# A two-layer retention and stick-breaking trunk: three runs of small moves in the order of issue

## The chip, the cores and the metric

The kernel runs on one core of a Trainium2 chip. A core has a matrix engine (TensorE, in profiles PE, with PEld for its weight loads), two elementwise engines (VectorE, DVE, and ScalarE, ACT), a general one (GpSimd, POOL) and SyncE (SP), which here only issues transfers (DMA). Each engine works through a queue of its own in a fixed order, and they wait for one another by semaphores. The metric is device time in microseconds (us), from start to end of one execution, lowest is best.

## The reference

One sequence of 1024 tokens of width 1024 passes through two layers in float32. Cut to what is computed:

```python
# layer 0: retention, 4 heads, q and k of 256, v and gate of 512 each
proj = rms_norm(h, g_pre) @ ret_w_in
q, k = rope(q), rope(k) * 256 ** -0.5
o = retention_chunkwise(q, k, v)          # sum over s <= t of gamma**(t-s) (q_t.k_s) v_s
o = (o - mean(o)) * rsqrt(var(o) + eps)   # per head and token
h = h + rms_norm((o * silu(g)) @ ret_w_out, g_post)
# one shared K and V from layer 0's output
k_sh, v_sh = split(rms_norm(h, g_kv) @ w_kv)
# layer 1: stick-breaking attention, 8 heads of 128 (values of 256)
q, g = split(rms_norm(h, g_sb) @ sb_w_in)
A[t, s] = sigmoid(z_ts) * prod(1 - sigmoid(z_tj) for s < j < t)   # s < t
h = h + rms_norm(((A @ v_sh) * silu(g)) @ sb_w_out, g_sbpost)
```

## The kernel before

**Arithmetic.** Every large product is done in a reduced matmul type with a split of each operand into a high and a low part: `split` (L514 on ACT takes the high part, L515 on DVE the rest), and `mm3` (L413 to L415) issues high x high, high x low and low x high into one PSUM bank. Tokens are worked in two halves of 512. The large input projections (classes `Feature` and `Values`) use a scheme of the Strassen kind: seven products, numbered 1, 2, 5, 6, 7, 3, 4, instead of eight block products, with sums and differences of the two token halves and of weight blocks as operands. A product of `Feature` comes in two pieces (e = 0, 1) of 4 x 3 matmuls, and a piece ends in additions (L888) or copies (L884) that empty its bank.

**Filling products.** A `Phase` lists products in an order, and makes the weight tiles (`whl`, 3 buffers) two ahead. At the end of both layers' projections a few products are left out of that list's main part and kept as `filler`: pieces that are dealt among the steps of the first heads, so that TensorE has work while a head waits. In layer A these are six pieces, product 2 of the projections of retention heads 1, 2 and 3, two pieces each: they give the first token half's queries of those heads, which go to DRAM (`qa`) and come back for the rotation. They add to sums kept in `sg` (heads 1 and 2, 4 buffers, which the gates' loads share) or `acc` (head 3). In layer C they are eight pieces: products 2 and 3 of the last two gate projections.

**Retention heads.** Eight head steps run, four heads for each token half. `Ret.scores` loads and rotates keys and queries (L635 to L638), turns the keys (`kt`, L648) and makes scores. `Ret.mix` makes the output blocks and the carried state and normalises each block: statistics on DVE (L731, L732, L734), reciprocal root on POOL, scaling on ACT (L750). `Ret.gate` multiplies with the gate (L766), transposes on TensorE (L770) and splits into `oT`. `outs` makes the output product of a head, in 16 half pieces, whose matmuls read all of that head's `oT`. In the loop of `layer_a` head n's mix and gate are merged with head n-1's output product and head n+1's scores; head 0 has no output product before it, and has the filler instead.

**Opening of layer C.** `P.marks` gives `first`, the number of the opening's chunks (20): products 1 and 2 of three key and query projections and of one value projection. Chunks 12 to 15 are product 1 of the values, 16 to 19 product 2, into banks po and pz. Work is hung at the end of chunks by number (`at`). The rest of the residual update and the row that scales the second token half (`c_stats`, L508) hang at chunks up to 14. `w_turn` has four steps, one for each quarter of the width: each scales the kept half with that row (L1566), makes sums and differences of token halves (L864, L865, L867, L868) and splits five results (L514, L515); product 5 of the values, chunk 20, reads the first (`oT`).

**Attention heads.** 16 head steps. `Att.rows` makes score rows (bank z, L1262 and L1263 on ACT, L1267 and L1268 on POOL, a scan L1270 and a product L1271 on DVE), `Att.mix` transposes them (L1298), splits them and multiplies them with values into banks po; its last step is the gate (L1326).

**What sets the order.** The program order isn't the order of the queues. At the end `arrange` takes all instructions, with a model of their times, and plans each engine's queue: `latest` gives each instruction a latest time, going back from the end, with TensorE's instructions chained in program order and each claim on a buffer chained to the reads of the tile that had it before; `place` then builds the queues from what is ready, earliest latest time first; `justify` takes new ranks from that plan, and of five rounds the one that ends first by the model is kept. Buffers of one tag are claimed in the order of first use in the program. So a move in program order changes TensorE's preferences and the claims on buffers, and what is ready at a time decides with them. The queues are fixed when the program is built; on the chip nothing is reordered.

Of the kernel before, what the change touches and what calls it, by code (L numbers as in the profile page):

```python
# [308 lines left out]
def trunk(ctx, tc, xT, wts, gains, trig, ident_in, cols, last_gain, out):  # L309
# [43 lines left out]
    def hl(tag):  # L353
        return S(tag, [2, 512], F32R)
# [191 lines left out]
    B, tabs = Ctx(), []  # L546
# [306 lines left out]
    def w_turn(raws, kept, scale):  # L853

        tags = {6: ["sgn", "sgn", "A", "ko"], 7: ["AT", "AT", "AT", "ko"], 4: ["v"] * 4}
        B.x1, B.T = [None] * 4, {n: [None] * 4 for n in (5, 6, 7, 4)}

        def make(kt):
            q = [raws[kt][:, 0], kept[kt][:, 0], raws[kt][:, 1], kept[kt][:, 1]]
            if kt == 0:  # L860
                B.late, B.far = S("qk", [4, 2, 512], F32R), S("oT", [4, 2, 512], F32R)
            scale(kt)
            B.x1[kt] = B.late[:, kt]
            V.tensor_tensor(q[0], q[1], q[0], ALU.subtract)  # L864
            V.tensor_tensor(q[1], q[3], q[1], ALU.subtract)  # L865
            split((B.x1[kt][:, 0, :], B.x1[kt][:, 1, :]), q[3])
            V.tensor_tensor(q[3], q[3], q[0], ALU.subtract)  # L867
            V.tensor_tensor(q[2], q[2], q[3], ALU.subtract)  # L868
            for n, r in ((5, q[0]), (6, q[3]), (7, q[1]), (4, q[2])):
                x = B.T[n][kt] = B.far[:, kt] if n == 5 else hl(tags[n][kt])  # L870
                split((x[:, 0, :], x[:, 1, :]), r)

        return [lambda kt=kt: make(kt) for kt in range(4)]
# [603 lines left out]
    def layer_a():  # L1477

        units = units_c()
        ready = units[3]  # L1480

        F, load, stats0, norm, later, stats1, scale = a_open()
        vg = [values_a(h, h < 2, F if h == 0 else None) for h in range(NH)]
        qk = [Feature(16 * h, None, put_raw(h), "last" if h else "", h and (lambda e, h=h: S("acc" if h == 3 else "sg", [512]),),
                      (None, "mb", "ma", "mb")[h]) for h in range(NH)]
        order = [(x, n) for x in vg[:2 + 1] for n in (1, 2)]
        opening = len(order)
        order += [(x, n) for x in [vg[2]] + vg[:2] for n in rest]
        order += [(x, n) for x in vg[2 + 1:] for n in full]
        qks = len(order)  # L1490
        order += [(qk[0], n) for n in full] + [(x, n) for x in qk[1:] for n in (1, 5, 6, 7, 3, 4)]
        fill = len(order)
        order += [(x, 2) for x in qk[1:]]
        P = Phase(order, (opening, qks, fill))
        first, kq, end, halt = P.marks
        at = P.at
        load[0]()
        at[0] += [late_constants] + load[1:4]
        at[1] += load[4:7]
        at[2] += load[7:]  # L1500
        for j, k in ((3, 0), (4, 1), (5, 2)):
            at[j].append(stats0[k])
        for j, k in zip((6, 6, 7, 7, 8, 9, 10, 11), range(8)):
            at[j].append(norm[k])
        for j, k in zip((8, 8, 9, 9, 10, 10, 11, 11), range(8)):
            at[j].append(later[k])
        for j, k in zip((12, 13, 14), range(3)):
            at[j].append(stats1[k])
        for j, f in zip((16, 18, 20, 21), w_turn(F.raws, F.kept, scale)):
            at[j].append(f)  # L1510
        at[first].append(lambda: trays.__setitem__(slice(None), ["sc0", "sc1", "A", "A", "A", "A"]))
        at[kq].append(lambda: ring.__setitem__(slice(None), ["wraw", "wraw", "wraw", "vo", "vo"]))
        heads = [Ret(t, h) for t in range(2) for h in range(NH)]
        sc = []
        for k in range(8):
            at[end - 4 + k // 2].append(lambda k=k: (sc or sc.extend(heads[0].scores()), sc[k]()))
        for f in P.pieces(0, end):
            f()
        filler = P.pieces(end, halt)
        ys, acc, kept, post, load = [], [], [], [], []  # L1520
        for n in range(8):
            H = heads[n]
            if n % 4 == 1:
                ys = []
            if n:
                pre, out = heads[n - 1].out(ys, acc if n == 4 else None)
                pre[0]()
            else:
                out = filler
                ring[:] = ["wraw"]  # L1530
            extra, late_extra, soon = [], [], [ready.pop(0) for _ in range(min(2, len(ready)))] if 0 < n < 7 else []
            if n == 5:
                post = a_post(0, y_d[0], acc)
            if 5 <= n < 7:
                extra = post[:6] if n == 5 else post[6:11]
            if n == 7:
                extra = post[11:] + c_stats(0)
                load = w_prep()
                late_extra = load[:4]
            sides = heads[n + 1].scores() if n < 7 else []  # L1540
            main = H.mix() + H.gate()
            merge(main, (out, 0, 1 if n else 3), (sides[:2], 0, len(main) - 5), (sides[2:], 5, 0), (extra, 1, 5 if n == 7 else 2), (late_extra, len(main) - 4, 0), (soon, 2, 3))
        acc = []
        pre, out = heads[7].out(ys, acc, kept)
        pre[0]()
        return units, out, load[4:], kept, a_post(1, y_d[0], acc, kept)

    def layer_c(units, out, load, kept, post):

        kq, gs, vs, _ = units  # L1550
        order = [(x, n) for x in kq[:3] + [vs[0]] for n in (1, 2)]
        opening = len(order)
        order += [(x, n) for x in [vs[0]] + kq[:3] for n in rest]
        order += [(x, n) for x in kq[3:] + [vs[1]] + gs[:2] for n in full]
        order += [(x, n) for x in gs[2:] for n in (1, 5, 6, 7, 4)]
        fill = len(order)
        order += [(x, n) for n in (2, 3) for x in gs[2:]]
        P = Phase(order, (opening, fill))
        first, end, halt = P.marks
        at = P.at  # L1560
        merge(out[:14], (load, 0, 2))
        P.ensure(1)
        merge(out[14:])

        def scale(kt):
            V.tensor_tensor(kept[kt][:], kept[kt][:], rowh[0][:].unsqueeze(1).broadcast_to([128, 2, 512]), ALU.mult)  # L1566
        post += c_stats(1)
        for j, k in zip((1,2,3,3,4,5,6,7,8,9,10,12,13,14), range(len(post))):
            at[j].append(post[k])
        for j, f in zip((first - 2, first - 1, first - 1, first - 1), w_turn(B.raws, kept, scale)):  # L1570
            at[j].append(f)
        trays[:] = ["sc0", "sc1", "A"]
        at[first].append(lambda: trays.__setitem__(slice(None), ["sc0", "sc1", "A", "A", "A", "A"]))
        at[first].append(lambda: ring.__setitem__(slice(None), ["wraw", "wraw", "wraw", "vo", "vo"]))
        pres = w_out()
        for k, f in enumerate(pres):
            at[first + 30 + (end - first - 30 - 28) * k // len(pres)].append(f)
        heads = [Att(t, p) for t in range(2) for p in range(NPAIR)]

        def rows_of(n):  # L1580
            return heads[n // 2].rows(n % 2) if n < 16 else []
        r0 = []
        for k in range(4):
            at[end - 4 + k].append(lambda k=k: (r0 or r0.extend(rows_of(0)), r0[k]()))
        for f in P.pieces(0, end):
            f()
        filler = P.pieces(end, halt)
        merge(heads[0].mix(0), (filler[:4], 0, 1))
        merge(rows_of(1), (filler[4:6], 0, 0))
        merge(heads[0].mix(1), (filler[6:], 0, 1), (rows_of(2), 0, 1))  # L1590
        ys, acc = [], []
        for n in range(2, 16):
            A = heads[n // 2]
            if n % 2 == 0:
                L = heads[n // 2 - 1]
                if n % 8 == 2:
                    ys = []
                pre, out = L.out(ys, acc if L.t == 0 and L.pr == 3 else None)
                pre[0]()
            extra = []  # L1600
            if n == 9:
                post = c_post(0, y_d[1], acc)
            if 10 <= n < 14:
                extra = post[3 * n - 30:3 * n - 27]
            if n == 15:
                extra, last = finish(1, heads[7], ys)
            merge(A.mix(n % 2), (out[8 * (n % 2):][:8], 0 if n % 2 else 1, 1), (rows_of(n + 1), 0, 1), (extra, 1, 1))
        last()
# [79 lines left out]
```

## Time and profile before

| what | value |
|---|---|
| median of 3 runs | 1631.67 us (1631.51 to 1632.08) |
| the profiled execution | 1631.42 us |
| its span, first to last instruction | 1629.4 us |
| mean granted clock of TensorE | 0.999 |
| DMA | 386.43 MB, mean 237 GB/s |

The profile is of one execution. Busy times are of instructions on an engine; a matmul's end is modelled, since matmuls are pipelined, so that the time from one start to the next is the pace, and a row's own duration is longer than that. In a row of the timeline stand the start, the duration, the engine, the line, the operation, the tile written and those read, the shapes and the count of merged instructions; in brackets the idle time of the engine ahead of it and what ended that. Tiles carry their tag's name (`pma`, `pmb`, `po`, `pz` are PSUM banks). A line can be a helper's: L515 is every split's low part, L360 every transfer.

### The profile page before, as it was taken

What the parts mean: (1) busy time and instruction counts of PE and PEld (TensorE: products, weight loads), DVE (VectorE), ACT (ScalarE), POOL (GpSimd) and SP (SyncE); (2) the same over time, 40 slices, a digit from 0 to 9 for tenths busy, and PEclk for the clock granted to TensorE, in tenths of its full rate; (3) what the DMA queues carried; (4) which work ended last, traced back from release to release, by engine and by line L of the source; (5) the groups of instructions that cost most, each with busy time, mean ns of one, the idle gap of its engine ahead of it and who ended that gap; (6) DMA issues with size and microseconds to landing.
All of it is one profiled execution on the core that took longest, in us unless ns stands there. A gap on an engine that the chain in (4) does not pass through costs nothing.

```text
span 1629.4 us, 22500 instructions
## 1 busy us (share of the span) xinstructions
PE 1620.4 (99%) x7659; PEld 1351.9 (83%) x7659; DVE 1219.4 (75%) x1956; ACT 803.8 (49%) x1535; POOL 122.7 (8%) x271
## 2 busy tenths in 40 slices
PE   9999999999999999999999999999999999999998
PEld 7888888888888888888878888888888888888887
DVE  8997866654668888887689877767658666878775
ACT  8553334433456555444356665566544433554432
POOL 0000000000012222221000000000001111010010
PEclk9999999999999999999999999999999999999999
DMA  8556765543387877784786788978337877869771
GB/s 319 188 179 247 249 212 186 209 141 135 110 277 229 308 262 271 247 286 147 246 273 224 258 312 289 342 279 308 119 127 262 305 276 264 281 212 333 251 273 52
DMA packets 175890, 386.43 MB, mean 237 GB/s; under 512 B 18080, under 2 KB 34592, under 8 KB 173216
## 3 DMA queue, kind: packets, MB, share of 16 engines
q1 hardware_dynamic: 175056, 383.93, 68.1%
q8 instruction: 60, 0.98, 0.2%
q10 hardware_dynamic: 720, 1.07, 0.2%
q14 instruction: 54, 0.44, 0.1%
HBM read 263.82 MB, written 121.11 MB: 236 GB/s over the span
## 4 chain that ended last, share of the span: by engine, by line
PE 97%; DMA 1%; ACT 1%; DVE 1%; issue 0%; SPq 0%; DVEq 0%; POOLq 0%; POOL 0%
PE pma L413 12%; PE pma L415 12%; PE pma L414 12%; PE pmb L413 9%; PE pmb L415 9%; PE pmb L414 9%; PE po L414 6%; PE po L415 6%; PE po L413 6%; PE pz L415 3%; PE pz L414 3%; PE pz L413 3%; PE pz L1298 2%; PE pz L770 1%; DMA wraw<-in_wts_dram 1%
## 5 line engine op out<-in xcount | busy, mean ns | idle before, releaser
L514 ACT ACTIVATE whl<-wraw 128x512 fp32r<-128x512 f32 x266 | 156.4, 625 | 180.8 <-issue 62.6
L515 DVE TENSOR_TENSOR whl<-wraw,whl 128x512 fp32r<-128x512 f32 x266 | 176.3, 687 | 86.8 <-ACT whl L514 82.6
L1270 DVE TENSOR_TENSOR_SCAN sgn<-sgn 128x128 f32<-128x128 f32 (+3 forms) x64 | 86.6, 1353 | 18.0 <-POOL sgn L1268 18.0
L515 DVE TENSOR_TENSOR AT<-pz,AT 128x512 fp32r<-128x512 f32 (+1 forms) x96 | 51.1, 551 | 48.1 <-ACT AT L514 47.6
L514 ACT ACTIVATE AT<-pz 128x512 fp32r<-128x512 f32 (+1 forms) x96 | 45.0, 492 | 67.9 <-PE pz L1298 66.9
L413 PE MATMUL pmb<-oT,whl 128*128 128x512 f32 x192 | 76.0, 396 | 0.0
L415 PE MATMUL pmb<-oT,whl 128*128 128x512 f32 x192 | 75.3, 392 | 0.0
L414 PE MATMUL pmb<-oT,whl 128*128 128x512 f32 x192 | 75.0, 391 | 0.0
L413 PE MATMUL pmb<-qk,whl 128*128 128x512 f32 x184 | 72.6, 394 | 0.0
L415 PE MATMUL pmb<-qk,whl 128*128 128x512 f32 x184 | 72.1, 392 | 0.0
L414 PE MATMUL pmb<-qk,whl 128*128 128x512 f32 x184 | 71.8, 390 | 0.0
L515 DVE TENSOR_TENSOR whl<-vo,whl 128x512 fp32r<-128x512 f32 x62 | 41.6, 687 | 34.8 <-ACT whl L514 34.6
L884 ACT ACTIVATE f<-pma 128x512 f32<-128x512 f32 x52 | 30.7, 595 | 51.2 <-PE pma L415 48.7
L514 ACT ACTIVATE whl<-vo 128x512 fp32r<-128x512 f32 x62 | 37.5, 624 | 33.4 <-PE pma L415 17.1
L413 PE MATMUL pma<-xh,whl 128*128 128x512 f32 x136 | 53.1, 391 | 0.0
L415 PE MATMUL pma<-xh,whl 128*128 128x512 f32 x136 | 53.1, 390 | 0.0
L414 PE MATMUL pma<-xh,whl 128*128 128x512 f32 x136 | 52.9, 389 | 0.0
L907 ACT ACTIVATE wraw<-wraw,gn 128x256 f32<-128x256 f32 x102 | 45.6, 497 | 12.7 <-DMA wraw<-in_wts_dram 11.6
L1267 POOL TENSOR_SCALAR_AFFINE_SELECT A<-A 128x128 f32<-128x128 f32 x32 | 11.0, 344 | 536.2 <-DMA ko<-k 396.0
L1263 ACT ACTIVATE sgn<-pz 128x512 f32<-128x512 f32 (+2 forms) x96 | 46.8, 489 | 0.0
L1262 ACT ACTIVATE xh<-pz 128x512 f32<-128x512 f32 (+3 forms) x48 | 23.6, 491 | 46.3 <-PE pz L415 46.1
L1262 ACT ACTIVATE A<-pz 128x512 f32<-128x512 f32 (+3 forms) x48 | 23.5, 490 | 42.0 <-PE pz L415 41.9
(580 smaller groups left out, 5138.3 us busy)
## 6 DMA issues: line engine op xcount, KB each, us to landing
wraw<-in_wts_dram SPq DMA_DIRECT2D x332, 256.0 KB, 3.8
whl<-w SPq DMA_DIRECT2D x56, 512.0 KB, 5.8
vo<-in_wts_dram SPq DMA_DIRECT2D x70, 256.0 KB, 4.3
xh<-k SPq DMA_DIRECT2D x32, 512.0 KB, 6.6
v<-v SPq DMA_DIRECT2D x32, 512.0 KB, 5.4
k<-A SPq DMA_DIRECT2D x21, 512.0 KB, 5.0
e<-whl SPq DMA_DIRECT2D x10, 1024.0 KB, 6.3
whl<-e SPq DMA_DIRECT2D x10, 1024.0 KB, 6.5
```

The lines of the kernel that those rows point to most:

```text
L413: MM(p, lh, rh, start=start, stop=False, **kw)
L414: MM(p, lh, rl, start=False, stop=False, **kw)
L415: MM(p, ll, rh, start=False, stop=stop, **kw)
L514: A_.activation(dst[0], src, AF.Copy)
L515: V.tensor_tensor(dst[1], src, f32(dst[0]), ALU.subtract)
L770: nc.tensor.transpose(pt[:, 128 * e:128 * e + 128], on[:, 128 * e:128 * e + 128], ident[:])
L884: A_.activation(c[:], p[:], AF.Copy)
L907: A_.activation(x, x, AF.Copy, scale=gcol(self.gains[col], 2 * (2 * i + k) + c))
L1262: A_.activation(a[:, o:o + ww], p[:, :ww], AF.Sigmoid)
L1263: A_.activation(n[:, o:o + ww], p[:, :ww], AF.Sigmoid, scale=-1.0)
L1270: V.tensor_tensor_scan(n[:, :W][:, ::-1], n[:, :W][:, ::-1], n[:, :W][:, ::-1], 1.0, ALU.mult, ALU.bypass)
L1298: nc.tensor.transpose(p[:, 128 * tb:128 * tb + 128], self.A[hh][tb][:, c0:c0 + 128], ident[:])
```

## The change

Three edits, each in the order of issue; no instruction is added or removed.

In `layer_a` the six filling pieces are dealt in another way: two are issued ahead of head 0's mix, one is merged into head 0's mix and gate, and the last three are put ahead of head 0's output product, in head 1's step. Before, all six were merged into head 0's step, one each behind steps 1, 2, 3, 5, 6 and 7 of its eleven (counted from 0).

```diff
                 pre, out = heads[n - 1].out(ys, acc if n == 4 else None)
                 pre[0]()
+                if n == 1:
+                    out = filler[-3:] + out
             else:
-                out = filler
+                out = filler[2:-3]
                 ring[:] = ["wraw"]
+                for f in filler[:2]:
+                    f()
```

In `layer_c` the four steps of `w_turn` hang at the last four chunks of the opening, 16 to 19, one each. Before, one hung at chunk 18 and three at 19.

```diff
-        for j, f in zip((first - 2, first - 1, first - 1, first - 1), w_turn(B.raws, kept, scale)):
+        for j, f in zip((first - 4,first - 3,first - 2,first - 1), w_turn(B.raws, kept, scale)):
             at[j].append(f)
```

In `layer_c`, too, the first six of its eight filling pieces are dealt three to the first attention head's mix and three to the second head's score rows. Before it was four and two. The last two stay in the second head's mix.

```diff
-        merge(heads[0].mix(0), (filler[:4], 0, 1))
-        merge(rows_of(1), (filler[4:6], 0, 0))
+        merge(heads[0].mix(0), (filler[:3], 0, 1))
+        merge(rows_of(1), (filler[3:6], 0, 0))
         merge(heads[0].mix(1), (filler[6:], 0, 1), (rows_of(2), 0, 1))
```

## The prediction

> **What bounds the kernel now.** I read the page first, then whom TensorE waited for, then a table of its busy time in stretches of 20 us, and last the timeline around each stretch that isn't full. From the page, its head, its first part and the chain that ended last by engine:
>
> ```profile
> span 1629.4 us, 22500 instructions
> PE 1620.4 (99%) x7659; PEld 1351.9 (83%) x7659; DVE 1219.4 (75%) x1956; ACT 803.8 (49%) x1535; POOL 122.7 (8%) x271
> PE 97%; DMA 1%; ACT 1%; DVE 1%; issue 0%; SPq 0%; DVEq 0%; POOLq 0%; POOL 0%
> ```
>
> TensorE (PE) is busy in 1620.4 of 1629.4 us, so 9.0 us of the span is all that a new order could fill, and the change is only a new order: it adds and removes no instruction. The waits of PE (line, releaser, total, times, longest) and the stretches that the change may touch (us, then busy PE, PEld, DVE, ACT, POOL, then the granted clock, DMA share and GB/s) say where those 9.0 us are:
>
> ```profile
> PE pz L386 <- DVE f L384: 1.7, 1, 1.7
> PE pma L413 <- ACT oT L514: 0.9, 1, 0.9
> PE po L413 <- DVE f L888: 0.3, 1, 0.3
> ...
> 60.00:80.00 20.00, 20.00 (x90) 16.57 (x89) 19.34 (x33) 12.66 (x22) 0.00 (x0) 1.00 0.41 131
> ...
> 480.00:500.00 20.00, 19.14 (x112) 16.30 (x111) 19.44 (x32) 11.96 (x23) 6.71 (x10) 1.00 0.63 194
> ...
> 840.00:860.00 20.00, 19.65 (x86) 15.72 (x85) 19.56 (x32) 11.40 (x21) 0.00 (x0) 1.00 0.46 172
> ...
> 1260.00:1280.00 20.00, 19.84 (x108) 16.72 (x107) 16.68 (x31) 9.05 (x24) 4.48 (x12) 1.00 0.92 330
> ...
> 1620.00:1640.00 20.00, 3.95 (x34) 3.71 (x33) 5.32 (x13) 1.75 (x6) 0.65 (x1) 0.90 0.14 53
> ```
>
> 1.7 us goes before the first matmul and about 5.4 us after the last (1629.4 - 1620.0 - 3.95): the change reaches neither. Inside, PE misses 0.86 us in 480:500 (the gate of retention head 0, part A below), 0.35 in 840:860 (the opening of layer C, part B) and 0.16 in 1260:1280 (the first attention heads, part C). Every edit has exactly one of these three holes behind it. Since everywhere else PE is full, a microsecond filled in a hole should come off the end, unless the new order opens another.
>
> **The change part by part.** A filling product is 12 matmuls of 128x512. Twelve such starts, in a stretch where PE waits for nothing, and one start after a group of transposes:
>
> ```profile
> 425.61 0.39 PE L413 MATMUL pmb<-oT,whl 128*128 128x512 f32 x1
> ...
> 428.33 0.39 PE L413 MATMUL pmb<-oT,whl 128*128 128x512 f32 x1
> ...
> 1238.47 0.47 PE L413 MATMUL pma<-xh,whl 128*128 128x512 f32 x1
> 1238.79 0.39 PE L414 MATMUL pma<-xh,whl 128*128 128x512 f32 x1
> ```
>
> So (428.33 - 425.61) / 12 = 0.227 us from start to start, 2.72 us a product, and 0.32 - 0.227 = 0.09 us more for each place where transposes break the stream.
>
> **A: three products kept for retention head 1.** The end of head 0 in the timelines of PE, DVE and ACT:
>
> ```profile
> 487.64 0.45 PE L415 MATMUL pmb<-xh,whl 128*128 128x512 f32 x1
> 487.93 0.60 PE L770 MATMUL pz<-ident,sgn 128*128 128x128 f32 x4
> 489.39 0.50 PE L413 MATMUL pma<-oT,whl 128*128 128x512 f32 x1 [0.86 <-ACT oT L514]
> 489.73 0.28 PE L413 MATMUL pz<-xh,xh 128*128 128x256 f32 x1
> ...
> 475.94 0.70 DVE L731 BATCH_NORM_STATS2 small<-po 128x6 f32<-128x512 f32 x1 [1.88 <-PE po L415]
> 479.42 0.17 DVE L732 BATCH_NORM_AGGREGATE small<-small 128x2 f32<-128x6 f32 x1
> ...
> 485.28 0.78 ACT L750 ACTIVATE sgn<-po,small,small 128x512 f32<-128x512 f32 x1
> 488.75 0.59 ACT L514 ACTIVATE oT<-pz 128x512 fp32r<-128x512 f32 x1
> ```
>
> The last block of head 0 is in PSUM at about 475.9, is normalised only at 485.28, turned at 487.93, split at 488.75, and only then can head 0's output product start (489.39). Before that, PE runs out: the sixth and last filling product ended with the row at 487.64. The hole is worth the idle 0.86 plus the late next start (489.73 - 489.39 - 0.227 = 0.11), so **1.0 us**. The edit issues two products ahead of head 0, one inside it, and three behind its gates. What follows on PE is the same work; what changes is the priority: the planner ranks PE by program order, so the gates' transposes no longer stand behind the last products, and these are what is left to run while the last block is normalised. The chain from 475.9 to 489.3 is 13.4 us long though its own steps (0.70, 0.17, 0.78, 0.60, 0.59 and the like) are some 5; the rest is queueing behind head 1's work, so 1 us can be found. I take the whole 1.0 us. Bounds: 0 (the products are used up as early as before) and -1.0.
>
> Costs that are hidden. Call the six products f0 to f5, two each for heads 1, 2 and 3. Keeping f3 back holds one of the 4 sg buffers longer, so the fourth gate's load must take the buffer of the first. It is needed at the L766 of 486.16, and the first gate reads its own 17 us sooner:
>
> ```profile
> 468.82 0.68 DVE L766 TENSOR_TENSOR sgn<-sgn,sg 128x512 f32<-128x512 f32 x1
> 486.16 0.68 DVE L766 TENSOR_TENSOR sgn<-sgn,sg 128x512 f32<-128x512 f32 x1
> ...
> sg<-ga SPq DMA_DIRECT2D x11, 256.0 KB, 3.6
> S<-q SPq DMA_DIRECT2D x10, 256.0 KB, 4.4
> ...
> 515.89 0.60 ACT L651 ACTIVATE vo<-pz 128x512 fp32r<-128x512 f32 x1 [1.18 <-PE pz L648]
> ```
>
> At 3.6 us a load that is free. The result of f3 goes out over SP's queue and comes back for head 2's rotation; moved by two or three products (5 to 8 us) and with 4.4 us a transfer it is back near 495 to 500, while head 2's keys are turned only at 515 (the L651 above). SP issues in its planned order, so a store that isn't ready holds what is behind it: the next weight loads, which have six wraw buffers of lead. With more than some 15 us of delay head 2 would start late. The weight tile (whl, 3 buffers) of f2 and f3 is held longer too, and the second output unit waits for it: that unit is first read four half products (5.4 us) into the output product, which itself starts behind f3. All three at nothing.
>
> **B: sums asked for sooner.** The four steps of w_turn move in program order from chunks 18, 19, 19, 19 to 16, 17, 18, 19. Their DVE work and the place where PE waits:
>
> ```profile
> 831.01 2.36 DVE L1566 TENSOR_TENSOR v<-v,acc 128x1024 f32<-128x1024 f32 x2 [1.33 <-ACT acc L508]
> 847.61 0.68 DVE L515 TENSOR_TENSOR oT<-A,oT 128x512 fp32r<-128x512 f32 x1
> 848.21 0.68 DVE L888 TENSOR_TENSOR f<-po,f 128x512 f32<-128x512 f32 x1
> 849.41 0.68 DVE L888 TENSOR_TENSOR f<-po,f 128x512 f32<-128x512 f32 x1
> ...
> 845.61 0.39 PE L415 MATMUL po<-whl,xh 128*128 128x512 f32 x1
> 848.33 0.39 PE L415 MATMUL pz<-whl,xh 128*128 128x512 f32 x1
> 849.03 0.47 PE L413 MATMUL po<-whl,oT 128*128 128x512 f32 x1 [0.32 <-DVE f L888]
> 849.54 0.50 PE L414 MATMUL po<-whl,oT 128*128 128x512 f32 x1
> ```
>
> From 848.33 two starts take 0.70 and 0.51 where 0.227 each is the pace: 0.47 + 0.28 = **0.75 us**. They wait for two L888, which empty the po banks and stand behind the sums in DVE's full queue: the last matmul into po ended at 846.0, the first L888 began at 848.21, right after a split. The sums can't begin sooner than the row that scales them (L508 ends at 831.0, DVE takes L1566 at once), so the edit moves claims on buffers and the planner's ranks, not data; the steps issue no DMA. The two additions could have run 2 us sooner ahead of a split (oT of the fourth step) whose reader comes three chunks (36 matmuls, 8.2 us) later, so there is room to get it right, and nothing in the edit that forces it: between 0 and -0.75 I take half, -0.4. The other way, the third step's A buffer is now claimed ahead of the value store of chunk 19, which may hold that store and its f buffer; six f buffers stand between that and PE, so I cost it at nothing.
>
> **C: products dealt 3-3.** One product (f3) moves from the first attention head's mix to the score rows of the second. The hole behind:
>
> ```profile
> 1274.05 0.45 PE L415 MATMUL pmb<-oT,whl 128*128 128x512 f32 x1
> 1274.54 0.33 PE L413 MATMUL pz<-xh,xh 128*128 128x128 f32 x1
> ...
> 1275.09 0.41 PE L1298 MATMUL pz<-ident,A 128*128 128x128 f32 x2
> 1275.62 0.39 PE L413 MATMUL pz<-xh,xh 128*128 128x256 f32 x1
> ```
>
> 0.49 instead of 0.227, and 0.53 instead of two transposes and their break (2 x 0.11 + 0.09 by the row above): 0.26 + 0.22, so **0.5 us**. It lies 30 us behind the moved product, with a whole mix between, and is a wait for a score's bank and operands, not for a filling product. The product's loads, weight tile and stores move by less than 3 us with it, and no other part of this stretch has a hole that they could widen. Half again: -0.25; bounds 0 and -0.5.
>
> **New order elsewhere.** All queues behind an edit are planned anew; one to three transpose breaks more or fewer (0.09 each) and a new hole of the size of the smaller ones: between -0.3 and +0.7, taken as +0.3.
>
> Sum: -1.0 - 0.4 - 0.25 + 0.3 = -1.35. The profiled execution took 1631.42 us (2.0 around its span), 0.25 below the median of the runs, 1631.67; on the median that gives 1630.3, and I say **1630.4**.
>
> **The rivals.**
> 1. The holes stay or come back beside their old place (the plan is a list of readiness, and a filling product that is ready is still used whenever the rest isn't): 1631.7, within 1631.2 to 1632.4. For it: the three products were ready and were used before the gates because the mix of head 0 has waits of its own. Chance 0.33.
> 2. All three holes close and nothing opens: 1631.67 - 1.0 - 0.75 - 0.5 = 1629.4. Chance 0.07.
> 3. Slower: PE's queue is fixed when the program is built, so a transpose of a gate (L770) that stands ahead of the kept products blocks them if its input is late. Place: 476 to 489, where head 0's last block took 9.3 us to L750. Up to three products, 8.2 us, would then stand behind the wait; it decides once over 4.3 us of them do (3.3 net of part A). Then 1635 to 1639. Against it: the planner puts what is ready first, and other heads' scores lie between. Chance 0.05; a smaller loss of the kind, 1632.4 to 1635, 0.04. [...]
> 4. Much faster: the pace itself would have to change. [...] A new order could still save breaks: 3.3 us less 2.25 from the holes is twelve breaks of 0.09, all gained. Chance 0.01.
>
> The forecast has 0.50 (1629.6 to 1631.2). 0.2%, about what a measurement of this kernel can tell from no change, is 3.3 us: more than all three holes together (2.25). So faster 0.01, same 0.94, slower 0.05. The range 1629.2 to 1632.2 takes in rival 2, most of rival 1 and the forecast, over 8 in 10.
>
> **What would show it.** A: no PE wait for oT before head 0's output product, kept products between the last L770 and it. B: no PE wait on L888 near 848, both L888 ahead of the last oT split. C: PE 20.00 in 1260:1280. Matmul count 7659 and clock 1.00 as before. I am wrong if PE's idle time inside the span rises above 1.4 us, or falls without the span doing so.

## The result and the profile after

| | before | after |
|---|---|---|
| median | 1631.91 us (22 runs, 1631.22 to 1635.22) | 1629.36 us (22 runs, 1628.69 to 1631.11) |
| span of the profiled execution | 1629.4 us | 1626.7 us |

The ratio is 0.9983, 95% interval 0.9977 to 0.9988: 2.55 us less by the medians, a small gain that lies inside the 0.2% called "same" in the prediction and inside its range, but below its forecast's band (1629.6 to 1631.2), and twice what it forecast. From the page of the changed kernel, the same three lines as before:

```profile
span 1626.7 us, 22505 instructions
...
PE 1619.3 (100%) x7659; PEld 1351.5 (83%) x7659; DVE 1219.1 (75%) x1956; ACT 804.1 (49%) x1535; POOL 122.1 (8%) x271
...
PE 98%; DMA 1%; DVE 0%; issue 0%; ACT 0%; SPq 0%; DVEq 0%; POOLq 0%; POOL 0%
```

The matmuls are the same 7659, and outside PE's busy time 7.4 us are left of 9.0. The waits of PE in the changed kernel:

```profile
PE pz L386 <- DVE f L384: 1.7, 1, 1.7
PE pma L414 <- DVE whl L515: 0.2, 1, 0.2
PE pma L415 <- DVE xh L515: 0.2, 1, 0.2
```

The waits for oT (L514) and on L888 are gone. The three stretches, and the last one (us, busy PE, PEld, DVE, ACT, POOL, clock, DMA share, GB/s):

```profile
480.00:500.00 20.00, 20.00 (x106) 17.06 (x105) 19.06 (x33) 11.51 (x21) 5.66 (x10) 1.00 0.78 275
840.00:860.00 20.00, 20.00 (x89) 16.25 (x88) 19.50 (x32) 12.15 (x24) 0.00 (x0) 1.00 0.41 150
1260.00:1280.00 20.00, 20.00 (x112) 17.46 (x112) 12.92 (x24) 8.96 (x23) 3.92 (x12) 1.00 0.85 297
1620.00:1640.00 20.00, 1.41 (x13) 1.17 (x11) 3.06 (x7) 0.51 (x2) 0.65 (x1) 0.94 0.11 41
```

PE is full in all three, and has 1.41 us of work past 1620 instead of 3.95: 2.54 us came off the end.

Busy time hides part of a hole, because a matmul's modelled end runs over the next one's start (a row of 512 columns is 0.39 us long, and the next starts after 0.227). A sharper count is PE's **lost time**: for each matmul, the time to the next start less the pace of its width (0.227 us for 512 columns, 0.174, 0.119 and 0.11 for 384, 256 and 128), summed over a stretch. It counts the breaks at transposes too, so only differences matter. The heads of the columns are the stretches, in us from the start; the entries are us:

| kernel | 2:40 | 465:500 (A) | 843:852 (B) | 1268:1278 (C) |
|---|---|---|---|---|
| before | 3.21 | 0.98 | 0.91 | 0.95 |
| after | 3.01 | 0.05 | 0.27 | 0.17 |

That is -0.93 for A, -0.64 for B, -0.78 for C, and -0.20 from the first 40 us, which the change doesn't touch: 2.55 of the 2.7 us between the spans. No new hole stands against it in this execution, which is the fastest of the 22.

**A.** Rows of PE, ACT and DVE of the changed kernel:

```profile
487.13 0.39 PE L413 MATMUL pmb<-xh,whl 128*128 128x512 f32 x1
487.35 0.39 PE L413 MATMUL po<-A,sc 128*128 128x512 f32 x1
...
488.95 0.60 PE L770 MATMUL pz<-ident,sgn 128*128 128x128 f32 x4
...
491.23 0.39 PE L414 MATMUL pmb<-xh,whl 128*128 128x512 f32 x1
...
484.25 0.78 ACT L750 ACTIVATE sgn<-po,small,small 128x512 f32<-128x512 f32 x1
...
489.58 0.60 ACT L514 ACTIVATE oT<-pz 128x512 fp32r<-128x512 f32 x1 [2.06 <-PE pz L770]
...
469.82 1.21 DVE L635 TENSOR_TENSOR S<-S,tab 128x1024 f32<-128x1024 f32 x1
```

Head 0's chain did not end earlier. Its last block is normalised 1.0 us sooner (L750 at 484.25 instead of 485.28), but the transposes of that gate stand behind kept products and head 1's output blocks in PE's queue (488.95), and its last split is at 489.58, where it was at 488.75. What changed is that PE still has work then. Kept products run up to 487.13 and again from 491.23, two matmuls, and head 1's output blocks (po<-A) already run at 487.35: head 1's query comes earlier (the rotation L635 at 469.82), because the two products that make it are issued ahead of head 0. In the timeline of the kernel before, that rotation was

```profile
476.56 1.21 DVE L635 TENSOR_TENSOR S<-S,tab 128x1024 f32<-128x1024 f32 x1
```

**B.** The same kernel near 848:

```profile
846.38 0.68 DVE L888 TENSOR_TENSOR f<-po,f 128x512 f32<-128x512 f32 x1
...
847.34 0.40 PE L413 MATMUL po<-whl,oT 128*128 128x512 f32 x1
...
847.58 0.68 DVE L888 TENSOR_TENSOR f<-po,f 128x512 f32<-128x512 f32 x1
847.71 0.50 PE L414 MATMUL po<-whl,oT 128*128 128x512 f32 x1
...
849.97 0.68 DVE L515 TENSOR_TENSOR oT<-A,oT 128x512 fp32r<-128x512 f32 x1
```

Both L888 are now ahead of the last oT split. One late start is left: 847.34 to 847.71 is 0.37 where 0.227 is the pace.

**C.** Where small score matmuls and transposes followed one another late before, 512-wide products stand between them now:

```profile
1274.08 0.47 PE L413 MATMUL po<-AT,v 128*128 128x512 f32 x1
1274.40 0.39 PE L414 MATMUL po<-AT,v 128*128 128x512 f32 x1
1274.63 0.40 PE L415 MATMUL po<-AT,v 128*128 128x512 f32 x1
1274.86 0.34 PE L413 MATMUL pz<-xh,xh 128*128 128x384 f32 x1
1275.04 0.40 PE L413 MATMUL pma<-oT,whl 128*128 128x512 f32 x1
```

### The profile page after: what moved, and what is told of

It is laid out like the page before. It is cut to its first block, busy times and chain, and to the rows that moved or that the text cites. A ratio compares the mean times of both kernels' runs of the same rounds, so it can differ in the third digit from the quotient of the medians.

```text
span 1626.7 us, 22505 instructions
## 1 busy us (share of the span) xinstructions
PE 1619.3 (100%) x7659; PEld 1351.5 (83%) x7659; DVE 1219.1 (75%) x1956; ACT 804.1 (49%) x1535; POOL 122.1 (8%) x271
## 3 DMA queue, kind: packets, MB, share of 16 engines
q10 hardware_dynamic: 720, 1.07, 0.2%
## 4 chain that ended last, share of the span: by engine, by line
PE 98%; DMA 1%; DVE 0%; issue 0%; ACT 0%; SPq 0%; DVEq 0%; POOLq 0%; POOL 0%
PE pma L413 12%; PE pma L415 12%; PE pma L414 12%; PE pmb L413 9%; PE pmb L415 9%; PE pmb L414 9%; PE po L414 6%; PE po L415 6%; PE po L413 6%; PE pz L414 3%; PE pz L415 3%; PE pz L413 3%; PE pz L1298 2%; PE pz L770 1%; PE pz L488 0%; DMA wraw<-in_wts_dram 0%
## 5 line engine op out<-in xcount | busy, mean ns | idle before, releaser
L514 ACT ACTIVATE whl<-wraw 128x512 fp32r<-128x512 f32 x266 | 156.2, 625 | 175.1 <-issue 62.6
L515 DVE TENSOR_TENSOR whl<-wraw,whl 128x512 fp32r<-128x512 f32 x266 | 176.1, 686 | 87.0 <-ACT whl L514 84.4
L515 DVE TENSOR_TENSOR AT<-pz,AT 128x512 fp32r<-128x512 f32 (+1 forms) x96 | 51.1, 551 | 50.0 <-ACT AT L514 49.6
L514 ACT ACTIVATE AT<-pz 128x512 fp32r<-128x512 f32 (+1 forms) x96 | 45.1, 492 | 68.4 <-PE pz L1298 67.9
L515 DVE TENSOR_TENSOR whl<-vo,whl 128x512 fp32r<-128x512 f32 x62 | 41.7, 689 | 35.1 <-ACT whl L514 34.8
L884 ACT ACTIVATE f<-pma 128x512 f32<-128x512 f32 x52 | 30.7, 595 | 49.7 <-PE pma L415 49.3
L514 ACT ACTIVATE whl<-vo 128x512 fp32r<-128x512 f32 x62 | 37.5, 624 | 34.7 <-PE pma L415 17.5
```

Source lines behind the costliest of these rows:

```text
L514: A_.activation(dst[0], src, AF.Copy)
L515: V.tensor_tensor(dst[1], src, f32(dst[0]), ALU.subtract)
L884: A_.activation(c[:], p[:], AF.Copy)
```

## The experiments

The theory after the result: each edit closes the hole behind it (A and C leave work for PE there, B lets DVE empty the banks sooner), and the three gains add. Rivals: the parts need one another; part A only moves its hole; another piece of an edit does the work than the one supposed. The kernels compute the reference in full; only the order differs, and in one of them a buffer. A theory's number holds within its own text. Medians (of 11 runs) are beside 33 runs of the kernel before on the same chip: its median was 1632.28 us for A, B, C and the hoist alone, 1632.01 for the pairs and for the step of the sums, 1632.26 for two kept products, the changed kernel once more, the other buffer and the 2-4 deal.

**Part A alone.** The first diff above, without the others.

> Only the retention edit (two products ahead of head 0, one inside, three kept for head 1); layer C as before. Theory 1, each edit closes the hole behind it and the effects add: TensorE's 0.86 us wait for oT near 488 is gone, the holes near 848 (0.75 us) and 1274 (0.5 us) are as before; span 1.0 to 1.1 us below before, ratio 0.9993 to 0.9994. Rival, the whole plan is made anew by any edit and the gain belongs to none of them alone: the holes near 848 or 1274 change too, and the span falls by something else than 1.0 us.

Measured: 1631.48 us, ratio 0.9997 (0.9988 to 1.0006); the span of its profile is 1629.5 us, and not the 1.0 us less that theory 1 expected. The wait for oT is gone, but there is another. From its waits of PE:

```profile
PE po L413 <- ACT sc L709: 0.5, 1, 0.5
PE po L413 <- DVE f L888: 0.3, 1, 0.3
```

And its timeline of ACT:

```profile
472.17 0.60 ACT L709 ACTIVATE sc<-po 128x512 f32<-128x512 f32 x1 [1.56 <-DMA st<-sc]
```

L709 copies a block of head 0's carried state into `sc`, of which there is one buffer, and SP stores it. The copy of the second block waits here until the store of the first has landed, holds a po bank meanwhile, and PE waits for that bank. Up to layer C each engine's queue in this program is the changed kernel's own, and there the same copy waited for nothing but PE (0.83 us). So it was open whether this belongs to the change or to this execution; more executions of the same queues had to tell.

**Part B alone.** The second diff.

> Only the sums of w_turn asked for sooner. Theory 1: the hole near 848 shrinks from 0.75 us to about 0.15, as in the changed kernel; the other two stay (0.86 us wait near 488 exactly as before); span 0.6 us less, ratio 0.9996. Rival: the edit moves no data and the hole near 848 closes only because everything ahead of it was planned anew by the retention edit; then this kernel has the hole still, ratio 1.0000.

Measured: 1631.85 us, ratio 0.9998 (0.9990 to 1.0007). Lost time at B 0.30 against 0.91; the wait for oT (0.9) and the hole at C are as before. The first 40 us lost 1.4 us more than in the profile of the kernel before, which hides the 0.6 in the span (1630.0). The hole still closes without part A, so the rival (it closes by what was planned ahead of it) falls.

**Part C alone.** The third diff.

> Only the 3-3 deal of the first attention heads. Theory 1: TensorE is full from 1260 to 1280, the late starts of 0.5 us are gone and some 0.3 us more by fewer breaks at transposes; span 0.8 us less, ratio 0.9995. Rival: the hole near 1274 stays or is replaced by another of its size, ratio 1.0000, since the gain in the changed kernel came from the new plan ahead of it.

Measured: 1631.59 us, ratio 0.9997 (0.9988 to 1.0006), span 1628.6, the 0.8 us less that theory 1 expected. Lost time at C 0.13 against 0.95; A and B are not closed (1.15 and 0.87).

**The hoist without the kept products.** Is it the two products ahead of head 0 that close A's hole, or those kept behind it?

```diff
-                out = filler
+                out = filler[2:]
+                for f in filler[:2]:
+                    f()
```

> Half of the retention edit: two products ahead of head 0, the other four merged into head 0 as before, none kept. If the gain of part A is the earlier queries of head 1 (its rotation, scores and mix come sooner and fill the wait), the 0.86 us wait is gone here too, span 1.0 us less, ratio 0.9994. If it is the products kept back, the wait stays at 0.5 to 1 us and the ratio is 0.9998 to 1.0000.

Measured: 1634.13 us, ratio 1.0009 (1.0000 to 1.0018), above the kernel before. The wait of PE that replaces the one for oT:

```profile
PE pz L770 <- DVE sgn L766: 1.7, 1, 1.7
```

Its timeline:

```profile
488.62 0.77 ACT L750 ACTIVATE sgn<-po,small,small 128x512 f32<-128x512 f32 x1
489.52 0.68 DVE L766 TENSOR_TENSOR sgn<-sgn,sg 128x512 f32<-128x512 f32 x1
490.32 0.42 PEld L770 LDWEIGHTS pz<-ident,sgn 128*128 128x128 f32 x4 [1.85 <-issue]
490.35 0.63 PE L770 MATMUL pz<-ident,sgn 128*128 128x128 f32 x4 [1.74 <-DVE sgn L766]
```

With nothing kept, PE comes to the last gate's transpose 1.7 us before its input is there. This is a wait of the kind of the prediction's third rival, in the gate it named, with no kept products behind it; it comes with the hoist and goes with the kept products. Neither alternative of the expectation was right: the hole did not close and did not stay, it grew. The two products that make head 1's query are ahead of head 0 here too, so an early query alone isn't enough. In that stretch the granted clock stayed at 1.00.

**Two products kept instead of three.**

```diff
-                    out = filler[-3:] + out
+                    out = filler[-2:] + out
...
-                out = filler[2:-3]
+                out = filler[2:-2]
```

> Part A with two of the six products kept instead of three; the third is merged into head 0's step, parts B and C left out. Theory 1 (what counts is how many matmuls are left on TensorE until head 0's first oT is split): in the changed kernel the split ended at 490.2 and the kept products at 491.5, so with one product less (2.72 us) TensorE runs out 1.3 to 2.0 us early, the wait for oT or for a transposed gate near 488 comes back at 1 to 2 us, and the time is 0.3 to 1.3 us above the kernel before. Theory 4 (the two products ahead of head 0 and the free gates do it, the number kept doesn't matter): no wait near 488 and 0.8 to 1.05 us below the kernel before.

Measured: 1633.25 us, ratio 1.0003 (0.9995 to 1.0012). Its wait of PE at 492.64:

```profile
PE po L413 <- ACT sgn L750: 1.2, 1, 1.2
```

The profile is of the longest of its eleven executions (1634.79 us), so its span says little.

A hole of the expected size came back, for another reason than the two named: PE waits for a po bank that ACT's scaling of a block has still to empty. The theory that the number kept doesn't matter falls by that wait; the median, 0.99 us above the kernel before where it wanted 0.8 us or more below, points the same way, though its interval reaches that far. Four products kept wasn't tried, nor three kept without the hoist.

**The parts in pairs.**

> Parts A and B, the attention products left 4-2. Theory 1 (each edit closes the hole behind it, the gains add): TensorE has no wait for oT near 488 and none on L888 near 848 beyond 0.25 us, the stretch 1260 to 1280 is as before (19.84), and the time is 1.05 + 0.60 = 1.65 us below the kernel before. Theory 2 (part A moves its hole, as in the run of A alone, where TensorE waited 0.47 us for ACT's L709 at 472): that wait is there again, and the time is about 0.1 + 0.6 = 0.7 us below. Theory 3 (the parts need one another): something between 2.0 and 2.7 us below.

> Parts A and C, the sums of token halves left where they were. Theory 1: no wait near 488, 20.00 busy in 1260 to 1280, the wait on L888 near 848 as before (0.3 us in the waits), and the time 1.05 + 0.85 = 1.9 us below the kernel before. Theory 2: the wait for L709 at 472 is there again, about 0.1 + 0.85 = 0.95 us below. With the run of A and B this gives two more executions of the same queues up to 500 us: if the wait at 472 comes in some and not in others, it goes by when the state's store lands and not by the plan.

> Parts B and C, the retention products left as before. Theory 1: the wait for oT near 488 is 0.9 us as before, the two other holes are closed, and the time is 0.60 + 0.85 = 1.45 us below the kernel before. Theory 3 (the parts need one another): less than 1.0 us below, with a hole of 0.3 us or more that neither part alone had.

Measured: A and B 1630.41 us (ratio 0.9990, 0.9981 to 0.9999); A and C 1630.64 (0.9991, 0.9982 to 1.0000); B and C 1630.62 (0.9991, 0.9982 to 0.9999). Lost time in us, worked out as above, in the profiles whose stretches lie at nearly the same times:

| kernel | 2:40 | 465:500 (A) | 843:852 (B) | 1268:1278 (C) |
|---|---|---|---|---|
| A | 3.42 | 1.05 | 0.88 | 0.99 |
| B | 4.65 | 0.92 | 0.30 | 0.95 |
| C | 3.26 | 1.15 | 0.87 | 0.13 |
| A, B | 4.40 | 0.41 | 0.32 | 0.97 |
| A, C | 3.62 | 0.27 | 0.88 | 0.15 |
| B, C | 3.68 | 0.95 | 0.29 | 0.16 |
| all (second profile) | 4.32 | 1.01 | 0.30 | 0.11 |
| all, second copy in f2 | 3.71 | 0.05 | 0.27 | 0.15 |
| B, second and third step only | 3.94 | 0.94 | 0.28 | 0.94 |

Columns B and C go with their own part and nothing else: 0.27 to 0.32 with it and 0.87 to 0.94 without; 0.11 to 0.17 and 0.94 to 0.99. (The three kernels that are left out lose 1.67 us at A with the hoist alone, 1.25 with two kept and 1.14 with the 2-4 deal.) So these gains add, and the theory that the parts need one another falls. The medians agree as far as they can: the three parts alone lie 0.80, 0.43 and 0.69 us below the kernel before, 1.92 together, the pairs 1.60, 1.37 and 1.39.

Column A doesn't follow its part alone: with the same queues up to 500 us it is 0.05, 0.27, 0.41, 1.01 and 1.05. That is 0.56 on average, where the kernels without part A lose 0.92 to 1.15, so over these five executions part A is worth some 0.4 us and not the 0.93 of the first profile. In both pairs with A, ACT waits for the state's store again (1.16 and 1.07 us).

**The changed kernel once more.**

> The changed kernel once more, on the same chip as the three others. Theory 1 (gains add): 2.5 us below the kernel before, holes near 488, 848 and 1274 closed as in its first profile. Theory 2: between 465 and 476 TensorE may lose up to 0.7 us to the store of the state as in the run of part A alone; with 0 in the first profile and 0.7 in that run, some 0.3.

Measured: 1630.53 us, ratio 0.9985 (0.9976 to 0.9994): 1.73 us below the kernel before, where theory 1 wanted 2.5 and the first measurement gave 2.55. The intervals overlap, so the two can't be told apart. The second copy of the state in this execution, PE's wait behind it, and the time from issue to landing of both stores:

```profile
473.36 0.60 ACT L709 ACTIVATE sc<-po 128x512 f32<-128x512 f32 x1 [1.82 <-DMA st<-sc]
474.01 0.50 PE L413 MATMUL po<-ko,xh 128*128 128x512 f32 x1 [0.73 <-ACT sc L709]
...
DMA to landing us min/median/max: 3.6/4.6/5.5
```

And in the first profile of the same kernel:

```profile
471.07 0.60 ACT L709 ACTIVATE sc<-po 128x512 f32<-128x512 f32 x1 [0.83 <-PE po L415]
...
DMA to landing us min/median/max: 4.5/4.6/4.7
```

The same program waits in one execution and not in the other. In the first profile the first block's copy began at 465.79 and the second's at 471.07, 5.28 us later; copy (0.60) and store (4.5 to 4.7) take 5.1 to 5.3 of that, so the store lands with next to nothing to spare. When it takes 5.5, the copy is late, and PE loses 0.73 us. That expectation (0 or 0.7) holds, and the hole that A alone showed belongs to part A but not to each execution. It is part A that takes the slack away. In the kernel before, the two stores landed after

```profile
DMA to landing us min/median/max: 2.0/3.7/5.5
```

and the first of them was the one of 2.0: it was issued at 462.93, and the DMA share was 0.32 in the 2.9 us ahead of it and 0.60 in its own two. With part A the first store is issued at 466 to 468, behind loads of queries, gates and weights (six in the 2.4 us from 462.51 on, in the first profile, where the DMA share was 0.99 while it was on its way), and takes 4.5 to 5.5 us in the five executions; in four of them ACT waits for it, 1.07 to 1.82 us.

**The changed kernel with the second copy in another buffer.** Is the store's wait all of it, and is a kernel without it faster?

```diff
-                f = S("sc2", [512])
+                f = S("f2" if d else "sc2", [512])
```

> The changed kernel with one line more: in the first token half the second state block is copied into a buffer of the tag f2 (6 copies) instead of sc2 (one), so ACT's L709 at 472 no longer waits for the store of the first block. Theory 2b (the wait seen at 472 with part A alone, 1.56 us on ACT and 0.47 on TensorE, goes by when that store lands and costs up to 0.7 us in some executions): no idle time of ACT behind a DMA st<-sc, and the median is 0 to 0.5 us below that of the changed kernel run beside it. Rival: f2 is also what the additions use, so a later one waits for its buffer and a new hole of 0.3 us or more opens between 460 and 500; the time is then above that of the changed kernel.

Measured: 1629.90 us, ratio 0.9983 (0.9974 to 0.9992), beside 1630.53 for the changed kernel on that chip. The copy in its timeline of ACT:

```profile
471.72 0.60 ACT L709 ACTIVATE f<-po 128x512 f32<-128x512 f32 x1 [0.79 <-PE po L415]
```

The wait is gone, column A is 0.05, and no wait for an f2 buffer shows. It beats the kernel before; that it beats the changed kernel isn't settled: 0.63 us, a little more than was expected, lies well inside the two intervals.

**Which step of the sums does B's work.**

```diff
-        for j, f in zip((first - 2, first - 1, first - 1, first - 1), w_turn(B.raws, kept, scale)):
+        for j, f in zip((first - 2, first - 2, first - 2, first - 1), w_turn(B.raws, kept, scale)):
```

> Of the four steps of the sums only the third is moved, from chunk 19 to 18; the first stays at 18, the second goes along to 18, the fourth stays at 19. Theory 1b (what part B does is to let the third step claim its A buffer ahead of the value stores of the last chunk, which use that tag too, so that DVE's additions L888 are no longer behind the last split): both L888 stand ahead of the last oT split, TensorE's starts there lose 0.25 us instead of 0.75, and the time is 0.5 to 0.6 us below the kernel before, the same as with all of part B. Theory 1c (the earlier first and second steps give DVE its room): the wait on L888 stays at 0.3 us and the time is that of the kernel before.

Measured: 1631.76 us, ratio 0.9998 (0.9989 to 1.0007). Its stretch and its DVE rows:

```profile
840.00:860.00 20.00, 20.00 (x89) 16.23 (x88) 19.91 (x33) 11.12 (x22) 0.00 (x0) 1.00 0.46 176
```

```profile
848.29 0.68 DVE L888 TENSOR_TENSOR f<-po,f 128x512 f32<-128x512 f32 x1
...
849.49 0.68 DVE L888 TENSOR_TENSOR f<-po,f 128x512 f32<-128x512 f32 x1
...
851.88 0.68 DVE L515 TENSOR_TENSOR oT<-A,oT 128x512 fp32r<-128x512 f32 x1
```

The hole at B closes as with all of the edit (0.28), so moving two steps by one chunk is enough, and the earlier chunks 16 and 17 add nothing. That the cause is the third step's claim on an A buffer, ahead of the value stores, fits but is only argued: the second step moved along with it. The time doesn't show the 0.6 us by itself: 0.25 by the medians, where the interval of the ratio is 0.18% wide (2.9 us).

**Attention products dealt 2-4.**

```diff
-        merge(heads[0].mix(0), (filler[:4], 0, 1))
-        merge(rows_of(1), (filler[4:6], 0, 0))
+        merge(heads[0].mix(0), (filler[:2], 0, 1))
+        merge(rows_of(1), (filler[2:6], 0, 0))
```

> The attention products dealt 2-4 instead of 3-3, parts A and B left out. Theory 1c (a product moved from the first mix to the second head's rows is work left for the late starts at 1274, so one more moved doesn't help once they are closed and the first mix runs out instead): 20.00 busy in 1260 to 1280 as with 3-3, but a new hole of 1 us or more between 1236 and 1262, and the time is 0.2 to 1.2 us above the kernel before. Theory 5 (less filling in the first mix is simply better, since that mix never waited): no hole from 1236 to 1280 and the time 0.7 to 0.9 us below the kernel before, as with 3-3 alone.

Measured: 1633.18 us, ratio 1.0005 (0.9996 to 1.0013). The old place is full, and the next 20 us are not:

```profile
1260.00:1280.00 20.00, 20.00 (x112) 17.32 (x111) 14.02 (x26) 9.50 (x24) 4.50 (x14) 1.00 0.97 325
1280.00:1300.00 20.00, 18.70 (x100) 15.77 (x99) 10.73 (x19) 8.95 (x20) 1.69 (x6) 1.00 0.87 310
```

Its timeline there:

```profile
1281.98 1.23 DVE L1270 TENSOR_TENSOR_SCAN sgn<-sgn 128x512 f32<-128x512 f32 x1 [0.67 <-POOL sgn L1268]
1283.13 0.67 DVE L1326 TENSOR_TENSOR sg<-po,sg 128x512 f32<-128x512 f32 x1
...
1283.84 0.50 PE L413 MATMUL po<-AT,v 128*128 128x512 f32 x1 [1.30 <-DVE sg L1326]
```

The median, 0.92 us above the kernel before, is as expected, though its interval takes in no change; the place of the hole wasn't as expected: not the first mix ran out, but a gate (L1326), which empties a po bank, now stands on DVE behind a scan that waited for POOL. So 3-3 is not "less filling in the first mix is better"; with one product more moved, the 0.8 us is lost to another hole of 1.3.

## Why the prediction was half of it

The reading was right: PE is the bound, only its holes can be won, each edit closes the one behind it, A's not in every execution. The signs it named all came out (kept products after head 0's gates, though only two matmuls of them, both L888 ahead of the last oT split, 20.00 in 1260:1280, 7659 matmuls at a granted clock of 1.00). What failed was **the sum**, in three of its four terms, and most in C, which was measured too small and then halved.

- **A, -1.0 taken:** -0.93 in the profile, so the size was right. The reason was partly wrong. I expected head 0's chain to find a microsecond and its gates' transposes to be free of the last products; the last transposes stand behind kept products and head 1's blocks, the chain ended 0.8 us later, and the gain came from kept products and from head 1's blocks, whose query the hoisted products made early. I put the hoist down as a part of the deal only; the runs without kept products and with two show that the hoist alone doesn't close the hole. That nearly all of the 1.0 us showed was in part luck: over the five executions it was some 0.4.
- **B, -0.4 taken as half of 0.75:** -0.64. "Nothing in the edit that forces it" was the step that failed. The edit does change the order of DVE's queue, in every kernel that has it, and nearly all of the bound came. That it does so through the third step's claim on a buffer is argued, not shown.
- **C, -0.25 taken as half of 0.5:** -0.78. Two errors. The hole was measured by two late starts, 0.49 and 0.53, but the rows beside those I quoted show two more in the kernel before:

```profile
1274.81 0.27 PE L415 MATMUL pz<-xh,xh 128*128 128x128 f32 x1
...
1275.85 0.28 PE L414 MATMUL pz<-xh,xh 128*128 128x256 f32 x1
```

1274.81 to 1275.09 is 0.28 where 0.11 is the pace, and 1275.62 to 1275.85 is 0.23 where 0.119 is; the four make 0.8. And I called it a wait for a score's bank that the moved product couldn't reach 30 us later; the run of C alone shows that it reaches it (0.13 against 0.95).
- **New order elsewhere, +0.3:** 0 in the first profile. A hole of the kind does exist, in A's own stretch, the store of the state: 0.2 to 1.0 us in four of the five profiles with A and one `sc` buffer. None of the three hidden costs of A that the prediction put at nothing is this one: it weighed the loads, the stores and the weight tiles of the kept products, and not the store of the state. So the debit was right in kind, and was not paid in the execution that was profiled.

With the sizes of the first profile, -0.93 - 0.64 - 0.78, the sum is -2.35, and 1631.67 - 2.35 = 1629.3: the prediction's second rival, to which I gave 0.07. Of the forecast's shortfall against that sum, C made 0.53, the debit 0.30, B 0.24, and A -0.07. With the average of the executions for A (0.4), the sum is some -1.8, near the 1.73 of the second measurement; it is B and C that are larger than forecast in every profile that has them. Whether the 22 executions of the first measurement met the store's wait less often than the five that were profiled stays open.

The rivals: holes that come back (0.33) is what A's hole did in full in two of its five executions, A alone and the changed kernel's second; at B and C it did not happen with these edits, and with the 2-4 deal a hole of 1.3 us opened beside C's. The wait of the slower rival showed in the run that hoists and keeps nothing (1.7 us). On the fourth, the pace stayed at 0.227 us from start to start, and PEld is 83% of the span before and after (1351.9 of 1629.4 us, 1351.5 of 1626.7), while PE lost 2.5 us of holes. The waits and the time from start to start showed the size of the gain; neither busy share, of PE or of PEld, did.

## What to carry to other kernels

When one engine is the bound and the change only orders its work, list its holes by time from start to start, all late starts of each, before halving anything: busy time showed 0.16 of the 0.8 us at C. Filling work is worth most where a chain ends that nothing else covers, and it must be counted there in matmuls: three products closed the wait that was aimed at, two and none left one of 1.2 and 1.7 us. An execution can land on the good side of a transfer that has no slack (one profile of the changed kernel shows no wait for the store, the other 1.82 us on ACT and 0.73 on PE), so profile the same program twice before a wait is called the change's doing or not.

## What the runs showed of the hardware

- The start of this program varied: PE lost from 3.0 to 6.0 us between 2 and 40 us, over kernels in which PE's and SP's queues are the same there, more than the whole change is worth. In part it is the pace: from 2.31 us on, nine starts of 512 columns in the profile before and seven in that of the changed kernel follow 0.42 to 0.43 us apart instead of 0.227. In part it is waits of 0.2 to 0.6 us each for a copy (L884) and a low part (L515), between 17 and 19.1 us. Beside medians of 11 runs, 1.4 us could just be told from nothing, 0.8 could not.
- In the profile of two kept products the matmuls start 0.43 us apart once more, from 20.9 to 23.5 us, at a granted clock of 0.57 over the stretch, and PE loses 1.7 us (4.00 x (1 - 0.57)):

```profile
20.00:24.00 4.00, 4.00 (x14) 3.27 (x14) 3.25 (x9) 4.00 (x8) 1.41 (x1) 0.57 1.03 353
```

The only waits of PE between its first matmul and this stretch were of 0.6 and 0.3 us. In the profiles of the kernel before and of the changed kernel the granted clock is 1.00 from 20 to 24 us, and 19 matmuls stand there instead of 14.

- Two stores of 256 KB took 3.6 and 5.5 us from issue to landing within one execution (the changed kernel's second profile), and 2.0 and 5.5 in the kernel before, on a queue that also carried loads.
- Where PE waited 1.2 us (two kept) and 1.7 us (the hoist alone), the granted clock was 1.00 over 480:500 in both.
